# Where ScalarE's queue holds the transfers of constants at the start of an encoder kernel: in front of the splits of x, or traced behind them

## The chip, the cores and the metric

The kernel runs on one core of one Trainium2 chip. The metric is the device time of one execution in microseconds (us). The engines are named TensorE (PE, matrix products; its weight loads are PEld), VectorE (DVE), ScalarE (ACT), GpSimd (POOL) and SyncE (SP). Transfers between DRAM and the on-chip memory are issued by SyncE and ScalarE here.

## The reference

Two layers of an encoder over 256 tokens of width 1024, in float32. Each layer is a feed-forward half step, a token mixer, and a second feed-forward half step:

```python
x = x + 0.5 * swiglu(rms_norm(x, norm_ffn1[l]), ffn1_in[l], ffn1_out[l])
h = rms_norm(x, norm_mix[l])
proj = h @ w_in[l]      # RWKV-7 columns | attention columns | branch gates
...                     # o_a: bidirectional RWKV-7 scans; o_b: differential attention
y = jnp.einsum('bsgc,gcd->bsgd', branches, w_branch[l])
merged = jnp.sum(gates * y, axis=2)
x = x + merged @ w_out[l]
x = x + 0.5 * swiglu(rms_norm(x, norm_ffn2[l]), ffn2_in[l], ffn2_out[l])
```

`rms_norm(x, g)` is x times its gain g, divided by the root of the mean square of x over the features.

## The kernel before

Activations stay on chip with the feature in the partition: `x` has 8 feature tiles of 128 partitions by 256 tokens. Weights stream through once, in tiles of 128 x 1024 (512 KB). A product in float32 is made of three passes in the type float32r: each operand is split into a high and a low part (`xh`, `xl` of x; `wh`, `wl` of a weight tile), and `mm3` (L145 to L147) adds xh·wh, xl·wh and xh·wl.

`weights` (L131) issues a weight tile's transfer on SyncE into `wr` (three buffers), then ScalarE makes `wh` (L135, three buffers) and VectorE makes `wl` (L139, two buffers).

`x_ready` (L150) handles one feature tile of x. ScalarE writes gain · x into `xh` (L158), VectorE writes the rest into `xl` (L159), ScalarE squares x (L162 for the first tile, L165 for the others), and from the second tile on GpSimd adds the square to a sum (L166, the last statement). `rstd` (L169) takes the sum over features, forms the reciprocal root `rsT`, puts it on a diagonal with `ident` (L179), spreads it over the partitions with a matmul (L181), and ScalarE copies the outcome to `rs` (L183). The feed-forward multiplies each product by `rs` only when it reads the accumulator (L199), so that matmuls can start before `rs` is there; three accumulators (`acc`) exist.

`run` (L842) issues the transfer of the first layer's packed vectors `vec` on SyncE, calls `constants`, then `x_ready` for the 8 tiles with a lowered rank for the squares (XP = -300), and then the layers. `constants` (L98) fills `ones` and `mhalf`, issues x in two transfers (256 KB and 768 KB) and six transfers of constants, all on ScalarE's queue: `ident` (L108), the second layer's `vec` (L110), `masks` (L112), `cum` (L114), `dist` (L116) and `hind` (L118). The transfers `lora`, `lra` and `lng` of `rwkv_common` (L263 to L267) are on the same queue and are traced behind the first feed-forward stage.

The program's order is set by the planner of the framework (Tile). The code is traced into a list; the planner then walks through modelled time and gives each engine, of the instructions that are ready, the one of the highest rank, which by default is the place in the trace. `high_priority(n)` shifts the rank. `issue_after(i)` adds an order (no wait for completion) behind instruction `i` for those instructions traced in its block that run on the engine of `i`. Each engine then works its queue strictly in that order.

Of the kernel before, what the change touches and what calls it, by code (L numbers as in the profile page):

```python
"""Hybrid bidirectional encoder trunk: macaron SwiGLU halves around RWKV-7 and differential attention.

Activations stay feature-major on chip ([feature in partition, feature tile, token]); weights stream
once. Float32 products of the large matrices are carried by float32r passes over an exact split of
both operands into a high and a low part.
"""
# [19 lines left out]
D = 1024  # L26
S = 256
L = 2
KD = D // P
# [11 lines left out]
XP = -300  # L41
# [3 lines left out]

# tiles that share a place with others
PLACE = {"b0": "ar0", "b1": "ar1", "b2": "wt0", "b3": "wt1", "b4": "ab", "b5": "qb", "ak2": "x"}

# columns of the packed vectors
V_F1, V_MIX, V_F2, V_MU, V_A0, V_KK, V_KA, V_RK, V_LB, V_QG, V_KG, V_SG = (  # L50
# [4 lines left out]
class Trunk:  # L55
# [21 lines left out]
    def slot(self, tag, shape, dt=F32, half=False):  # L77
        """A tile of 8 KB (or 4) in a partition; tiles of one tag follow each other in place."""
        tag, n = PLACE.get(tag, tag), int(np.prod(shape[1:]))
        t = self.sp.tile([P, 1024 if half else 2048], dt, tag=tag, name=self.nm(tag))  # L80
        v = t[:, :n]
        names = "abcd"[:len(shape) - 1]
        if len(names) > 1:
            v = v.rearrange(f"p ({' '.join(names)}) -> p {' '.join(names)}", **dict(zip(names, shape[1:])))
        return v
# [13 lines left out]
    def constants(self):  # L99
        nc, io = self.nc, self.io  # L100
        self.ones = self.cp.tile([P, P], F32, name="ones")
        nc.vector.memset(self.ones, 1.0)
        self.mhalf = self.cp.tile([P, 32], F32, name="mhalf")
        nc.scalar.activation(self.mhalf, self.ones[:, 0:32], AF.Copy, scale=-0.5)
        self.ident = self.cp.tile([P, P], F32, name="ident")
        nc.scalar.dma_start(self.x[:, 0:2], io["x"][:, 0:2])
        nc.scalar.dma_start(self.x[:, 2:8], io["x"][:, 2:8])
        nc.scalar.dma_start(self.ident, io["c_ident"])  # L108
        for l in range(1, L):
            nc.scalar.dma_start(self.vec[l], io["vec"][l])  # L110
        self.masks = self.cp.tile([P, 6, 64], F32, name="masks")
        nc.scalar.dma_start(self.masks, io["c_masks"])  # L112
        self.cum = self.cp.tile([P, 2, 130], F32, name="cum")
        nc.scalar.dma_start(self.cum, io["c_cum"])  # L114
        self.dist = self.cp.tile([P, 384], F32, name="dist")
        nc.scalar.dma_start(self.dist, io["c_dist"])  # L116
        self.hind = self.cp.tile([P, 2], F32, name="hind")
        nc.scalar.dma_start(self.hind, io["c_hind"])  # L118
        self.da = self.cp.tile([P, S], F32, name="da")
        self.sdg = self.cp.tile([P, S], F32, name="sdg")  # L120
        self.lng = self.cp.tile([P, 4, 64], F32, name="lng")
        self.mu1 = self.cp.tile([P, 15], F32, name="mu1")
        self.mu2 = self.cp.tile([P, 15], F32, name="mu2")
        self.ka1 = self.cp.tile([P, 4], F32, name="ka1")
        self.kah = self.cp.tile([P, 4], F32, name="kah")
        self.a0h = self.cp.tile([P, 8], F32, name="a0h")

    # weights ------------------------------------------------------------------------------------
    def weights(self, src, n):
# [18 lines left out]

    # the residual and its norm ------------------------------------------------------------------
    def x_ready(self, l, g0, k, start, later=0):  # L150
        """Splits gain * x of one feature tile and adds its squares."""
        nc = self.nc
        x, g = self.x[:, k], self.vec[l][:, g0 + k:g0 + k + 1]
# [30 lines left out]

    # feed-forward half step ---------------------------------------------------------------------
    def ffn(self, l, w_in, w_out, nxt):
# [30 lines left out]

    # one tile of x @ W for two feature tiles, in a bank -----------------------------------------
    def project(self, w_in, tiles):
# [7 lines left out]
    def shifted(self, l, tiles, outs):  # L227
        """outs = p + mu * (centred_shift(p) - p) of RWKV column tiles."""
        nc, n = self.nc, len(tiles)
# [23 lines left out]

    # RWKV-7: everything that the scans need -----------------------------------------------------
    def rwkv_common(self, l):
        """The low-rank parts and the places of what the pairs of heads give."""
        nc, io, vec = self.nc, self.io, self.vec[l]
# [42 lines left out]
    def rwkv_kr(self, l, p):  # L300
        """Key and receptance of a pair of heads."""
        self.shifted(l, [4 + p, p], [self.kr[:, p, 0], self.kr[:, p, 1]])

    def rwkv_v(self, l, q):
        """Values of two pairs of heads, by token."""
        nc = self.nc
        v = self.tmp("vv", [P, 2, S], bufs=1)
        self.shifted(l, [8 + 2 * q, 9 + 2 * q], [v[:, 0], v[:, 1]])
        for i in range(2):
            ps = self.gen()  # L310
            for c in range(4):
                self.turn(ps[:, c * 64:c * 64 + 64], v[:, i, c * 64:c * 64 + 64])
            nc.scalar.activation(self.vt[:, 2 * q + i], ps[:, :S].rearrange("p (c s) -> p c s", c=4), AF.Copy)

    def rwkv_pair(self, p):
        """A pair of heads in both directions; the last part of the second direction waits for the next call."""
        st = self.pair_front(p, self.kr[:, p, 0], self.kr[:, p, 1])
# [15 lines left out]
    def turn(self, out, a):  # L333
        """out[h] = a[h].T for both halves of the partitions."""
        for h in range(2):
# [3 lines left out]
    def pair_front(self, p, k, r):  # L339
        nc, vec, mm = self.nc, self.vl, self.nc.tensor.matmul  # L340
        # kk = k * k_k; its squared norm's reciprocal by head goes into kk * iclr
        kk, sq = self.t1(), self.t1()
# [17 lines left out]
    def unit_front(self, p, d, st, sig, a2, da):  # L360
        nc, mm = self.nc, self.nc.tensor.matmul
        k, r, kk, bm, ks = st
        c4 = lambda t: t.rearrange("p (c s) -> p c s", c=4)
        # 2 * iclr - 1 = tanh of half the logit
        a, bw, kd = self.t1(), self.t1(), self.t1()
# [31 lines left out]
    def unit_back(self, p, d, st, bw, kw):  # L397
# [26 lines left out]
        if d == 1:  # L424
            # sum over a head of r * r_k * (k of both directions)
            ps = self.gen()
# [6 lines left out]

    # (I - A)^-1 of the 32 x 32 diagonal blocks, one in a partition ---------------------------------
    def invert(self, q):
# [24 lines left out]

        # 16 x 16 blocks, row by row from below: X[i, j:] = G[i, j:] X[j:, j:]
        D16 = 16 * 33
        nc.vector.tensor_copy(view(x, 14 * 32 + 15, (D16, 2), (1, 1)), view(g, 14 * 32 + 15, (D16, 2), (1, 1)))
        for i in range(13, -1, -1):
# [3 lines left out]
            add(view(x, i * 32 + j, (D16, 2), (1, n)), tm)  # L468
        # the block off the diagonal: X01 = X00 G01 X11, with X00 G01 in the place below G's diagonal
        for o in range(0, 16, 4):  # L470
# [18 lines left out]
    def merge_blocks(self, q):  # L489
        """The blocks off the diagonal: T = D + D A D."""  # L490
        nc, dt = self.nc, self.dt[q]
# [15 lines left out]

    # the scans, chunk by chunk --------------------------------------------------------------------
    def chain(self, l, q):
        """Two pairs of heads, both directions: the forward scan at chunk j, the other at chunk 3 - j."""  # L510
        nc, mm = self.nc, self.nc.tensor.matmul
# [96 lines left out]

    # differential attention -----------------------------------------------------------------------
    def att(self):  # L610
# [55 lines left out]
    def attention_core(self, l):  # L666
# [3 lines left out]
        for h in range(4):  # L670
# [13 lines left out]
            for m in range(2):  # L684
                for t in range(2):
                    nc.scalar.activation(lg[m][:, t], lg[m][:, t], AF.Exp, scale=slope, bias=mx[:, m, t:t + 1],
                                         accum_out=sm[:, m, t:t + 1])
            # e0 / s0 - lambda * e1 / s1 = (e0 - lambda * s0 / s1 * e1) / s0
            nc.vector.reciprocal(rs, sm)
# [30 lines left out]

    # the token mixer ------------------------------------------------------------------------------
    def gates(self, l, b):
        """2 * sigmoid - 1 = tanh of half the logits, kept in DRAM until the branch is ready; a step a feature tile."""
        nc = self.nc
# [31 lines left out]
    def gated(self, q, n0, r):  # L756
        """Weights of a filler: their split is queued behind the inversion's steps."""
        ops, n = self.inv[q], [0]
# [83 lines left out]
    def run(self, stages):  # L842
# [4 lines left out]
        self.constants()  # L847
        for k in range(KD):
            self.x_ready(0, V_F1, k, k == 0, XP)
        outf = lambda j: nc.scalar.dma_start(io["out"][:, j], self.x[:, j])  # L850
# [70 lines left out]
```

## Time and profile before

| | |
|---|---|
| time, median of 3 runs | 1410.89 us (1405.38 to 1413.88) |
| profiled execution, first to last instruction | span 1406.5 us (no time of its own is given beside it) |
| TensorE busy | 1349.9 us, 96% |
| VectorE, ScalarE, GpSimd busy | 67%, 47%, 20% |
| data moved | 227.60 MB, 162 GB/s mean |
| TensorE clock granted, mean | 0.987 |

A share of busy time is a mean over stages. The span has seven stages between the six instructions that write `rs`: a head of 27.1 us, and then feed-forward and mixer stages in turn.

### The profile page before, as it was taken

How to read it: one execution, taken by the hardware profiler on the slowest of the kernel's cores; microseconds unless marked ns; L12 is line 12 of the kernel's file. 1: busy time of each engine (PE TensorE's matmuls, PEld its weight loads, DVE VectorE, ACT ScalarE, POOL GpSimd, SP SyncE). 2: the span in 40 equal slices, each digit the busy share in tenths (PEclk: the TensorE clock that was granted, in tenths of full speed). 3: DMA queues.
4: the chain of work that ended last, by engine and by line, in shares of the span. 5: the costliest groups of instructions: out<-in, count | busy, mean ns of one | idle time of the engine just before them, and what ended most of it. 6: DMA issues, size and time to landing. Idle time of an engine off the chain costs nothing.

```text
span 1406.5 us, 30996 instructions
## 1 busy us (share of the span) xinstructions
PE 1349.9 (96%) x12916; PEld 1285.0 (91%) x12916; DVE 940.7 (67%) x1421; ACT 664.8 (47%) x1059; POOL 288.2 (20%) x284
## 2 busy tenths in 40 slices
PE   6999999998989999999999999999988999999999
PEld 6999998877889899999999999988767888999998
DVE  4655557799957766555556655588999577656644
ACT  5444445344444455444444444554543554544432
POOL 3111015445001112111111111154540010211100
PEclk9999999999999999999999999999999999999999
DMA  6555664325333565556655556633352445555564
GB/s 230 182 181 182 180 207 156 99 91 138 108 103 116 191 229 177 185 181 179 181 184 187 183 174 183 218 111 113 93 143 83 114 136 193 175 187 184 183 188 143
DMA packets 90333, 227.60 MB, mean 162 GB/s; under 512 B 29264, under 2 KB 35408, under 8 KB 89680
## 3 DMA queue, kind: packets, MB, share of 16 engines
q1 hardware_dynamic: 78640, 207.16, 47.0%
q10 hardware_dynamic: 11552, 18.46, 3.9%
q8 instruction: 101, 1.65, 0.5%
q14 instruction: 40, 0.33, 0.1%
HBM read 214.05 MB, written 11.53 MB: 160 GB/s over the span
## 4 chain that ended last, share of the span: by engine, by line
PE 80%; DVE 11%; DMA 3%; issue 2%; ACT 2%; POOL 2%; ACTq 0%; SPq 0%; DVEq 0%; POOLq 0%
PE acc L147 23%; PE acc L146 23%; PE acc L145 23%; DVE tv L458 3%; DVE wl L139 3%; DVE lora L459 2%; PE back L331 1%; PE gen L331 1%; PE att L679 1%; PE back L337 1%; PE gen L283 1%; DMA x<-xd 1%; DMA x<-x 1%; DMA f<-g 0%; PE acc L643 0%
## 5 line engine op out<-in xcount | busy, mean ns | idle before, releaser
L135 ACT ACTIVATE wh<-wr 128x1024 fp32r<-128x1024 f32 (+1 forms) x390 | 404.9, 1039 | 414.7 <-PE acc L146 268.6
L139 DVE TENSOR_TENSOR wl<-wr,wh 128x1024 fp32r<-128x1024 f32 (+1 forms) x390 | 475.5, 1219 | 171.0 <-PE acc L147 83.0
L145 PE MATMUL acc<-xh,wh 128*128 128x256 f32 x1904 | 540.2, 286 | 11.8 <-ACT wh L135 11.8
L146 PE MATMUL acc<-xl,wh 128*128 128x256 f32 x1904 | 539.5, 285 | 0.0
L147 PE MATMUL acc<-xh,wl 128*128 128x256 f32 x1904 | 529.9, 286 | 2.4 <-DVE wl L139 2.1
L145 PEld LDWEIGHTS acc<-xh,wh 128*128 128x128 f32 x1904 | 367.0, 193 | 17.3 <-ACT wh L135 12.0
L146 PEld LDWEIGHTS acc<-xl,wh 128*128 128x128 f32 x1904 | 367.0, 193 | 3.2 <-issue 2.5
L147 PEld LDWEIGHTS acc<-xh,wl 128*128 128x128 f32 x1904 | 360.6, 193 | 9.4 <-issue 3.5
L204 POOL TENSOR_TENSOR t<-t,t 128x256 f32<-128x256 f32 x88 | 89.3, 1016 | 403.7 <-ACT t L202 403.7
L145 PE MATMUL acc<-ar,wh 128*128 128x256 f32 x512 | 144.9, 283 | 0.0
L147 PE MATMUL acc<-ar,wl 128*128 128x256 f32 x512 | 144.9, 283 | 0.0
L199 DVE TENSOR_TENSOR t<-acc,rs 128x512 f32<-128x512 f32 x88 | 60.8, 692 | 119.7 <-PE acc L147 114.6
L146 PE MATMUL acc<-wt,wh 128*128 128x256 f32 x384 | 108.9, 284 | 0.0
L145 PEld LDWEIGHTS acc<-ar,wh 128*128 128x128 f32 x512 | 98.3, 192 | 0.0
L147 PEld LDWEIGHTS acc<-ar,wl 128*128 128x128 f32 x512 | 98.3, 192 | 0.0
L145 PE MATMUL acc<-wt,wh 128*128 128x256 f32 x320 | 91.0, 286 | 3.4 <-DVE x L839 2.2
L166 POOL TENSOR_TENSOR vv<-vv,t 128x256 f32<-128x256 f32 x42 | 36.8, 876 | 279.4 <-ACT t L165 271.8
L147 PE MATMUL acc<-wt,wl 128*128 128x256 f32 x320 | 91.5, 286 | 1.3 <-DVE wl L139 1.2
L458 DVE TENSOR_TENSOR tv<-lora 64x8 f32<-64x8 f32 (+10 forms) x88 | 74.9, 852 | 1.9
L146 PEld LDWEIGHTS acc<-wt,wh 128*128 128x128 f32 x384 | 74.4, 194 | 0.0
L146 PE MATMUL acc<-ab,wh 128*128 128x256 f32 x256 | 72.4, 283 | 0.0
L145 PEld LDWEIGHTS acc<-wt,wh 128*128 128x128 f32 x320 | 61.9, 194 | 4.0 <-issue 2.4
(234 smaller groups left out, 1935.1 us busy)
## 6 DMA issues: line engine op xcount, KB each, us to landing
wr<-f1i SPq DMA_DIRECT2D x88, 512.0 KB, 3.7
wr<-f2i SPq DMA_DIRECT2D x88, 512.0 KB, 3.6
wr<-win SPq DMA_DIRECT2D x62, 512.0 KB, 3.6
wr<-f1o SPq DMA_DIRECT2D x32, 512.0 KB, 3.6
wr<-f2o SPq DMA_DIRECT2D x32, 512.0 KB, 3.6
wr<-watt SPq DMA_DIRECT2D x24, 512.0 KB, 3.7
wr<-wbr SPq DMA_DIRECT2D x16, 512.0 KB, 3.6
wr<-wout SPq DMA_DIRECT2D x16, 512.0 KB, 3.4
```

The costliest lines, as they stand in the source:

```text
L135: nc.scalar.activation(wh[:, :n], raw[:, :n], AF.Copy)
L139: nc.vector.tensor_tensor(wl[:, :n], raw[:, :n], wh[:, :n].bitcast(F32), ALU.subtract)
L145: mm(out, wh, xh, start=first, stop=False)
L146: mm(out, wh, xl, start=False, stop=False)
L147: mm(out, wl, xh, start=False, stop=last)
L166: nc.gpsimd.tensor_tensor(self.sq, self.sq, sq, ALU.add)
L199: nc.vector.tensor_tensor(gu, ps.rearrange("p (a b) -> p a b", a=2), self.rs.unsqueeze(1).to_broadcast([P, 2, S]), ALU.mult)
L204: nc.gpsimd.tensor_tensor(h, s, gu[:, 1], ALU.mult)
L283: mm(ps, dw[r, t * P:(t + 1) * P], w2[r], start=True, stop=True)
L331: self.nc.tensor.matmul(out[r], a[r], b[r], start=start, stop=stop)
L458: mul = lambda o, a, b: ops.append(nc.vector.tensor_tensor(o, a, b, ALU.mult).ins)
L459: add = lambda o, a: ops.append(nc.vector.tensor_reduce(o, a, AX.X, ALU.add).ins)
```

## The change

The loop over `x_ready` moves from `run` into `constants`, behind the two transfers of x. The six transfers of constants (and the allocation of the tiles behind them) become a new function, `constants_late`, which is called behind the loop, in a block of `issue_after` with the last instruction traced so far. Nothing else changes but comments that are left out.

```diff
         nc.scalar.dma_start(self.x[:, 0:2], io["x"][:, 0:2])
         nc.scalar.dma_start(self.x[:, 2:8], io["x"][:, 2:8])
+        for k in range(KD):
+            self.x_ready(0, V_F1, k, k == 0, XP)
+        with self.tc.issue_after(nc.cur_bb.bb.instructions[-1]):
+            self.constants_late()
+
+    def constants_late(self):
+        nc, io = self.nc, self.io
         nc.scalar.dma_start(self.ident, io["c_ident"])
         for l in range(1, L):
             nc.scalar.dma_start(self.vec[l], io["vec"][l])
...
         self.constants()
-        for k in range(KD):
-            self.x_ready(0, V_F1, k, k == 0, XP)
         outf = lambda j: nc.scalar.dma_start(io["out"][:, j], self.x[:, j])
```

## Rows read from the trace of the kernel before

**Rows 1.** The page: busy us of each engine, and the chain that ended last.
```profile
PE 1349.9 (96%) x12916; PEld 1285.0 (91%) x12916; DVE 940.7 (67%) x1421; ACT 664.8 (47%) x1059; POOL 288.2 (20%) x284
...
PE 80%; DVE 11%; DMA 3%; issue 2%; ACT 2%; POOL 2%; ACTq 0%; SPq 0%; DVEq 0%; POOLq 0%
```

**Rows 2.** Stages: from:to, us, busy us (instructions) per engine, clock, DMA share, GB/s.
```profile
0.00:27.10 27.10, 14.74 (x98) 13.93 (x99) 12.38 (x23) 13.18 (x25) 8.40 (x12) 1.00 0.72 246
27.10:218.04 190.94, 190.94 (x1592) 190.89 (x1591) 109.44 (x131) 91.96 (x131) 31.75 (x32) 1.00 0.59 188
218.04:528.00 309.96, 292.62 (x3274) 260.81 (x3272) 249.71 (x448) 148.92 (x269) 81.10 (x78) 0.96 0.43 134
...
719.28:910.82 191.54, 191.54 (x1597) 191.49 (x1596) 110.17 (x131) 90.96 (x130) 30.38 (x32) 1.00 0.59 188
910.82:1223.31 312.49, 288.90 (x3275) 257.01 (x3274) 250.66 (x442) 148.55 (x269) 85.19 (x78) 0.98 0.42 129
```

**Rows 3.** Timeline of TensorE: start, us, instruction, idle time before it and its releaser.
```profile
11.06 0.58 PE L145 MATMUL acc<-xh,wh 128*128 128x256 f32 x1 [11.06 <-ACT wh L135]
...
12.32 0.58 PE L147 MATMUL acc<-xh,wl 128*128 128x256 f32 x1 [0.47 <-DVE wl L139]
...
17.80 0.38 PE L145 MATMUL acc<-xh,wh 128*128 128x256 f32 x1 [0.75 <-ACT wh L135]
```

**Rows 4.** Timeline of the queues of SyncE (SPq) and ScalarE (ACTq, ACT), the head.
```profile
0.73 0.42 ACTq L106 DMA_DIRECT2D x<-x  x1
...
1.17 31.15 SPq L133 DMA_DIRECT2D wr<-f1i  x10
...
1.25 0.39 ACTq L107 DMA_DIRECT2D x<-x  x1
...
3.94 0.33 ACTq L112 DMA_DIRECT2D masks<-c_masks  x1
...
7.83 0.34 ACTq L116 DMA_DIRECT2D dist<-c_dist  x1
8.77 0.33 ACTq L118 DMA_DIRECT2D hind<-c_hind  x1
9.15 0.51 ACT L158 ACTIVATE xh<-x,vec 128x256 fp32r<-128x256 f32 x1 [6.45 <-DMA x<-x]
9.54 0.33 ACTq L263 DMA_DIRECT2D lora<-w  x1
9.57 0.49 ACT L158 ACTIVATE xh<-x,vec 128x256 fp32r<-128x256 f32 x1
9.97 1.04 ACT L135 ACTIVATE wh<-wr 128x1024 fp32r<-128x1024 f32 x1
```

**Rows 5.** Transfers: queue, count, KB each, us from issue to landing.
```profile
wr<-f1i SPq DMA_DIRECT2D x1, 512.0 KB, 6.6
x<-x ACTq DMA_DIRECT2D x1, 256.0 KB, 3.2
...
x<-x ACTq DMA_DIRECT2D x1, 768.0 KB, 7.5
ident<-c_ident ACTq DMA_DIRECT2D x1, 64.0 KB, 8.6
...
wr<-f1i SPq DMA_DIRECT2D x88, 512.0 KB, 3.7
```

**Rows 6.** Timeline of VectorE: the diagonal (L179) and reads of accumulators (L199).
```profile
23.25 0.48 DVE L179 TENSOR_SCALAR t<-ident,rsT 128x128 f32<-128x128 f32 x2 [0.83 <-POOL rsT L176]
...
27.52 1.29 DVE L199 TENSOR_TENSOR t<-acc,rs 128x512 f32<-128x512 f32 x2 [1.73 <-ACT rs L183]
...
39.57 0.69 DVE L199 TENSOR_TENSOR t<-acc,rs 128x512 f32<-128x512 f32 x1 [1.08 <-PE acc L147]
...
45.33 0.69 DVE L199 TENSOR_TENSOR t<-acc,rs 128x512 f32<-128x512 f32 x1 [1.50 <-PE acc L147]
```

**Rows 7.** Instructions that read `hind`, the earliest: count, duration in ns, first to last start.
```profile
L347 PEld LDWEIGHTS gen<-hind,t x32: 186/192/192, 233.9 to 996.0; 128*128 128x128 f32 x32
```

## The prediction

> **What bounds the kernel now.** I read the page first, then the span cut into stages, and then only the first 40 us, where the change lies. The page [rows 1] shows TensorE busy for 1349.9 us, 96% of the span, and 80% of the chain that ended last is TensorE. The reader is to see that ScalarE (47%) and the transfers are not the bound, so a change to them pays only where TensorE is seen waiting.
>
> The stages [rows 2] are cut at the six instructions that write the row scale `rs` (L183). The first feed-forward stages of the two layers take 190.94 and 191.54 us with TensorE busy throughout. The two mixers take 309.96 and 312.49 us, with 17 and 24 us of TensorE idle. The head, up to the first `rs`, has TensorE busy for 14.74 of 27.10 us. So 12.4 us are missing there, and this is all that the change can reach directly; it is 0.9% of the span.
>
> What fills those 12.4 us: TensorE's first matmul is at 11.06 and waited for `wh`, the high part of the first weight tile; 0.47 and 0.75 us follow in two further gaps [rows 3]. So 11.06 us is the head of the program before TensorE has anything.
>
> ScalarE's timeline of that head [rows 4] has two transfers of x (0.73, 1.25), `ident` and the second layer's `vec`, `masks` (3.94), `cum`, `dist` (7.83), `hind` (8.77), and only then the first split `xh` at 9.15, a second at 9.57, and `wh` at 9.97 to 11.01. The issues are not slow (0.33 to 0.42 us each); they wait. The landing times [rows 5] say for what. The first part of x lands at 0.73 + 3.2 = 3.93, and `masks` starts at 3.94. The first weight tile, issued at 1.17 [rows 4], lands 6.6 us later at 7.8, and `dist` starts at 7.83. The second part of x lands at 1.25 + 7.5 = 8.75, and `hind` starts at 8.77. Eight transfers (vec, two of x, three of weights, `ident`, vec) are out by then; from the ninth on, each seems to start as an earlier one lands. ScalarE works its queue in order, so the split of the first two tiles of x, whose data was there at 3.93, starts 5.2 us later, behind `dist` and `hind`.
>
> **The change, part by part.** No instruction is added or removed. Six transfers (`ident`, `vec`, `masks`, `cum`, `dist`, `hind`; by their shapes 64 + 33 + 192 + 130 + 192 + 1 = 612 KB) are traced behind 8 `xh` and 8 squares on ScalarE, 8 `xl` on VectorE and 7 adds on GpSimd. The vec of layer 0 and the weight tiles on SP's queue keep their place.
>
> *Does the hold bind?* `issue_after(i)` orders those instructions of its block that run on the engine of `i`. The last one traced in front of the block is `x_ready`'s last statement, the add on GpSimd (L166); the six transfers are issued by ScalarE. So I read the hold as empty. What is left is trace order, a rank among instructions that are ready at one moment. The trace shows how much readiness outweighs it: `lora` (L263), traced a whole feed-forward stage later, is issued at 9.54, ahead of the second split [rows 4]. The constants need nothing, the splits need x. So `ident`, `vec` and probably `masks` and `cum` still go out first, and only what is left once the planner counts x as landed changes place with the first splits.
>
> *What it can give.* Nothing, if the order stays. If `xh` 0 and 1 pass `dist` and `hind`, but `wh` stays behind `hind`, `wh` starts where the first `xh` does now, 9.15 in place of 9.97: 0.8 us. If all constants leave the head, `wh` is bound by its own tile at 7.83, ends 1.04 us later at 8.87, and TensorE starts at 8.9: 2.2 us. Beyond that, the constants that are in flight before 7.83 (64 + 33 + 192 + 130 = 419 KB) could slow x and weights by at most their own time, 419 KB at the head's 246 GB/s [rows 2] = 1.7 us, so the gain is at most 3.9 us. TensorE's matmuls at 11.06 and 12.32 last 0.58 us, that at 17.80 lasts 0.38 [rows 3]; I take it that the slow stretch moves with the start. I take 0.8 us, as the row of `lora` says that ready transfers stay in front.
>
> *What it can cost.* Each issue takes up to 0.42 us of ScalarE's queue, six of them about 2.5 us. `lora`'s issue (9.54 to 9.87) overlaps the splits at 9.15 to 9.66 and 9.57 [rows 4], so an issue beside an ACTIVATE costs near nothing; I take 0, and keep 2.5 us as the other end. Behind a moved transfer stand the squares and the next `wh`, for one of which TensorE already runs dry at 17.80 [rows 3]. Without the cover of the ACTIVATEs these 2.5 us would go straight into that gap.
>
> *Who needs the constants.* `ident` alone is due early: it enters the diagonal at 23.25 [rows 6]. From there come `rs` at 27.1 and the reads of the first two accumulators at 27.52, over by 28.8. Three accumulators exist, and a product takes 5.76 us (45.33 − 39.57 [rows 6]); the fourth product, which is read at 39.57, thus starts near 33.8. So `ident` may come about 5 us late for free, near 28. It took 8.6 us to land at worst [rows 5], so it must be issued after 19.6 to cost anything. The other constants are first read at 233.9 or later [rows 7]. I take 0.
>
> The Trainium skill, DMA: Bandwidth & Descriptors, section Rules for kernel authors, says to issue a transfer early, compute, and wait for it late; the change does the opposite. By the rule the constants would only lose by moving. The 5 us under `ident` and 200 us under the rest say that this loss is covered here, and the rule takes no account of the issue standing in front of compute, which is the cost that [rows 4] show.
>
> *The rest of the program.* The planner places instructions by modelled time, so a shift at the head may turn the order of work 300 us later. The trace prices this: the same stage, planned anew in the other layer, differs by 0.6 us in the feed-forward halves and by 2.5 us in the mixers [rows 2]. Two mixers turned the same way are 5 us (an estimate from these two rows), of either sign. I take 0, since 190 us of a feed-forward stage with no TensorE gap lie between.
>
> **Sum.** The profiled execution has a span of 1406.5 us; the runs shown have a median of 1410.89 (1405.38 to 1413.88), 4.4 us more, so I apply the difference to the median. 1410.89 − 0.8 + 0 + 0 = 1410.1 us, with −3.9 and +2.5 us as the ends of the head alone. The three runs spread over 0.6% by themselves; 0.5% (7 us) is about what a measurement here can tell from no change.
>
> **Rivals.** *It does nothing.* The order at the head stays: 1410.9. For it: an empty hold, and transfers that are ready at once. Against it: x may count as landed before `dist`. *It does what it says.* All six go behind the splits: 1407.0 to 1408.7. For it: rows 4 show 5 us of blocked queue. Against it: the hold is on another engine. *Slower: late constants wait in the queue of the weight splits.* By then three weight tiles are always in flight, and a transfer that must wait for one to land waits up to 3.7 us, the median of the weight tiles [rows 5], holding the next `wh` back; TensorE then runs dry. One such wait is within the gap won at the start; from two uncovered waits on (7.4 us) it decides: 1418, and 1425 with four. Against it: `lora` was issued like this at 9.54, beside the splits, and TensorE's wait for the next `wh` was 0.75 us [rows 3, 4]. The Trainium skill's rule of issuing early (DMA: Bandwidth & Descriptors, Rules for kernel authors) stands on this rival's side. *The mixers turn over.* 1401 to 1421 for twice the 5 us above. For it: 41 us of idle TensorE there, set by the order; against it: the two layers agree within 2.5 us.
>
> **How the numbers follow.** Forecast (0 to 2.2 us gained at the head, the rest as before) 0.48; nothing 0.14; full gain 0.10; late constants 0.08; mixers turned 0.20. The first three (0.72) lie within 0.5%, less 0.03 that the spread of the runs may carry out of it (0.02 faster, 0.01 slower). Of the turned mixers I put 0.10 below −0.5%, 0.06 above and 0.04 between; of the late constants 0.06 above and 0.02 between. Faster 0.10 + 0.02 = 0.12, slower 0.06 + 0.06 + 0.01 = 0.13, same 0.69 + 0.04 + 0.02 = 0.75. The range runs to 1401 and 1420, 10 us each way, and leaves out the far ends of the turned mixers and three or more waits. The likeliest case's own range is 1407 to 1413.
>
> **What would show it.** In the head: the place of the first `xh` in ScalarE's queue against `dist` and `hind` (forecast: ahead of at least one of them, near 4 to 8 us), the first matmul between 8.9 and 11.1, the diagonal with `ident` still near 21 to 24 with no wait for a transfer. In the stages: feed-forward within 1 us of 191, mixers within 3 us of 310 and 312.5. The prediction is wrong if the mixers move by over 5 us together, if TensorE shows new waits for `wh` between 12 and 40 us, or if the six transfers sit as a block behind the last square, which would mean that the hold binds.

## The result, and the profile after

The changed kernel takes 1425.86 us (1424.47 to 1427.58, 4 runs) against 1408.99 us (1405.38 to 1413.88, 4 runs) of the kernel before: a ratio of 1.0127, interval 1.0098 to 1.0155. It is slower by 17 us, outside the range that was given. The profiled execution took 1424.47 us with a span of 1422.7.

The page of the kernel after, busy time of each engine and the chain that ended last (before: [rows 1]):

```profile
PE 1362.4 (96%) x12916; PEld 1295.2 (91%) x12916; DVE 929.8 (65%) x1421; ACT 664.0 (47%) x1059; POOL 295.6 (21%) x284
...
PE 77%; DVE 12%; DMA 5%; POOL 2%; issue 2%; ACT 1%; SPq 0%; ACTq 0%; DVEq 0%; POOLq 0%
```

The instructions are the same in number, and TensorE is still at 96%. The page hides the loss: TensorE's busy time rose by 12.5 us for the same 12916 matmuls, while the mean granted clock fell from 0.987 to 0.977. The Trainium skill (Trainium Kernel Development and Optimization, Performance Expectations) calls matmul busy time a bad metric for how close a kernel is to its roofline, because matmuls are pipelined. Here it is no measure of a change either, with 96% on both sides of a loss of 1.3%, and the weight loads (PEld), with 91% on both sides, show no more.

The stages of the kernel after, cut at the writes of `rs` as in [rows 2] (from:to, us, busy us and instructions of PE, PEld, DVE, ACT, POOL, clock, DMA share, GB/s):

```profile
0.00:26.31 26.31, 15.19 (x98) 14.40 (x99) 12.06 (x23) 13.40 (x24) 8.37 (x12) 1.00 0.76 252
26.31:217.25 190.94, 190.94 (x1592) 190.89 (x1591) 109.17 (x131) 92.06 (x130) 30.11 (x32) 1.00 0.60 189
217.25:543.26 326.01, 299.41 (x3275) 265.61 (x3274) 244.21 (x448) 148.27 (x269) 90.28 (x78) 0.94 0.42 127
...
734.21:925.80 191.59, 191.59 (x1597) 191.54 (x1596) 108.94 (x131) 90.69 (x130) 31.25 (x32) 1.00 0.60 188
925.80:1239.46 313.66, 294.51 (x3275) 262.25 (x3274) 247.77 (x442) 148.13 (x270) 82.72 (x78) 0.96 0.42 129
```

[rows 2] cut the first mixer of the kernel before at 528.00, but `rs` is written at 528.34. Cut there, as the other stages are, it reads:

```profile
218.04:528.34 310.30, 292.96 (x3275) 261.12 (x3274) 249.71 (x448) 148.92 (x270) 81.10 (x78) 0.96 0.43 134
```

The head gained 0.79 us (27.10 to 26.31), the feed-forward stages stand still, the second mixer lost 1.2 us, and the first mixer lost 15.7 us (310.30 to 326.01). There TensorE is busy 6.5 us longer (299.41 against 292.96, at a clock of 0.94 against 0.96) and idle 9.3 us longer (26.6 against 17.3). In the second mixer it is busy 5.6 us longer, at a clock of 0.96 against 0.98, but idle 4.4 us less. So the change worked where it was made, and the loss stands 200 us behind it, in a stage that none of the moved transfers feeds late: `hind`, the last of them, was issued at 8.69.

The head after, ScalarE and its queue (before: [rows 4]; line numbers behind L107 are higher by 7 in the code that did not move):

```profile
1.66 0.45 ACTq L115 DMA_DIRECT2D ident<-c_ident  x1
...
4.10 0.51 ACT L165 ACTIVATE xh<-x,vec 128x256 fp32r<-128x256 f32 x1 [1.39 <-DMA x<-x]
...
4.47 0.47 ACTq L119 DMA_DIRECT2D masks<-c_masks  x1
...
7.91 0.33 ACTq L123 DMA_DIRECT2D dist<-c_dist  x1
8.69 0.33 ACTq L125 DMA_DIRECT2D hind<-c_hind  x1
9.07 1.06 ACT L142 ACTIVATE wh<-wr 128x1024 fp32r<-128x1024 f32 x1 [4.07 <-DMA x<-x]
```

The first two splits now start at 4.10 and 4.51 and not at 9.15 and 9.57, as soon as their part of x is there. `ident` still goes out first. In the planned queue both splits stand in front of the other five constants (`vec` goes out at 4.11 and no longer at 2.14, the others within 0.7 us of their old times), and `wh` still stands behind `hind`. The hold of `issue_after` is empty, as read: the six are issued by 8.69, while GpSimd's adds, the last of which is named in the hold, run until 20.3, and without the hold the planned program is the same to the last instruction.

The planned program also tells what the issues wait for. The framework gives the transfers eight semaphores in turn, and the issue of a ninth transfer waits for the landing of the first: `masks` for the first part of x, `dist` for the first weight tile, `hind` for the second part of x. The 5 us of blocked queue [rows 4] are these waits; they show no limit of the chip. TensorE's first matmul comes at 10.18 and not at 11.06 [rows 3]:

```profile
10.18 0.58 PE L152 MATMUL acc<-xh,wh 128*128 128x256 f32 x1 [10.18 <-ACT wh L142]
```

Where the first mixer loses is seen in TensorE's own timeline near its end. The kernel before, the last products of attention and the transposes of its output `osb` (start, us, instruction, idle time before it and its releaser):

```profile
457.71 0.61 PE L702 MATMUL att<-va,f 128*128 128x128 f32 x4
...
460.40 0.63 PE L716 MATMUL att<-ident,osb 128*128 128x128 f32 x4 [0.54 <-DVE osb L713]
...
463.97 0.63 PE L716 MATMUL att<-ident,osb 128*128 128x128 f32 x4 [0.42 <-DVE osb L713]
```

The kernel after, the same instructions:

```profile
468.72 0.71 PE L709 MATMUL att<-va,f 128*128 128x128 f32 x4
474.11 1.08 PE L723 MATMUL att<-ident,osb 128*128 128x128 f32 x4 [4.68 <-DVE osb L720]
477.23 1.11 PE L723 MATMUL att<-ident,osb 128*128 128x128 f32 x4 [2.04 <-DVE icl L726]
```

Attention's last product comes 11 us later. Before, other matmuls stood between those rows; after, nothing stands there in TensorE's queue. TensorE waits 4.68 and 2.04 us, and a group of four transposes then takes 1.1 us in place of 0.63. From the first of them to 483.5 the granted clock is 0.50, the lower of its two levels (1.2 in place of 2.4 GHz):

```profile
474.00:483.50 9.50, 7.35 (x43) 6.53 (x44) 4.64 (x13) 1.79 (x3) 1.98 (x2) 0.50 0.20 72
```

The second place lies earlier. SyncE's queue around the second block inversion, first the kernel before, then the kernel after (`d<-ab` writes its input to DRAM, `lora<-d` reads it back regrouped, `d<-lora` writes the first inversion's result):

```profile
334.35 0.33 SPq L440 DMA_DIRECT2D d<-ab  x1
336.97 2.74 SPq L450 DMA_DIRECT2D lora<-d  x4
...
343.27 0.50 SPq L480 DMA_DIRECT2D d<-lora  x1
```

```profile
341.50 0.42 SPq L447 DMA_DIRECT2D d<-ab  x1
342.96 0.51 SPq L487 DMA_DIRECT2D d<-lora  x1
...
346.51 0.93 SPq L457 DMA_DIRECT2D lora<-d  x2
...
350.67 1.02 SPq L457 DMA_DIRECT2D lora<-d  x2
```

The second inversion's input comes 7 us later, and two of its four reads stand behind other transfers. Which of these differences costs the 17 us, and whether they come from the moved transfers or from the order, the experiments had to say.

### The profile page after: what moved, and what is told of

Its sections match the earlier page's. It is cut to its first block, busy times and chain, and to the rows that moved or that the text cites. A ratio compares the mean times of both kernels' runs of the same rounds, so it can differ in the third digit from the quotient of the medians.

```text
span 1422.7 us, 30989 instructions
## 1 busy us (share of the span) xinstructions
PE 1362.4 (96%) x12916; PEld 1295.2 (91%) x12916; DVE 929.8 (65%) x1421; ACT 664.0 (47%) x1059; POOL 295.6 (21%) x284
## 4 chain that ended last, share of the span: by engine, by line
PE 77%; DVE 12%; DMA 5%; POOL 2%; issue 2%; ACT 1%; SPq 0%; ACTq 0%; DVEq 0%; POOLq 0%
PE acc L154 23%; PE acc L153 22%; PE acc L152 22%; DVE tv L465 3%; DVE wl L146 3%; DVE lora L466 2%; PE back L338 1%; DMA x<-xd 1%; PE gen L338 1%; DMA lora<-d 1%; DMA wr<-win 1%; POOL n L664 1%; PE att L686 1%; DMA wr<-wout 1%; PE gen L290 1%
## 5 line engine op out<-in xcount | busy, mean ns | idle before, releaser
L153 PEld LDWEIGHTS acc<-wt,wh 128*128 128x128 f32 x384 | 75.2, 196 | 0.0
L154 PEld LDWEIGHTS acc<-wt,wl 128*128 128x128 f32 x320 | 62.8, 196 | 2.9 <-DVE wl L146 2.9
```

The lines of the kernel that those rows point to most:

```text
L153: mm(out, wh, xl, start=False, stop=False)
L154: mm(out, wl, xh, start=False, stop=last)
```

## The experiments

Where an order is pinned, a table lists for each engine the instructions traced behind the head in the order in which they are to be issued, and an order edge without a semaphore is put between each and the next:

```diff
+def pin(tc, traced, table):
...
+    info = mybir.DependencyInfo(mybir.DependencyClass.NoSync, mybir.DependencyReason.DATA)
+    for code in table.values():
+        places = ...   # one engine's instructions, by their place in the trace
+        for p, q in zip(places, places[1:]):
+            tc.add_manual_dep(traced[q], traced[p].name, info, reason="pin")
...
         Trunk(ctx, tc, io).run(stages)
+        pin(tc, list(nc.cur_bb.bb.instructions), ORDER)
```

**Head or order.** Two crossed kernels: e1 has the head of the kernel after and, from the first feed-forward stage on, the order of the kernel before; e2 has the head of before and the order of after.

> The changed kernel, with the issue order of every engine behind the head (all that is traced from the first feed-forward stage on) held to that of the kernel before. Theory P (the loss is the planner's other order in the first mixer; the moved transfers themselves gain 0.8 us at the head): ratio to the kernel before 0.998 to 1.001, first matmul near 10.2 us, first mixer 309 to 311 us. Theory T (the moved transfers themselves cost: later landing, other contention, or a lower clock that follows from them): ratio stays near 1.013 and the first mixer near 326 us.

> The kernel before with its head untouched, and the issue order behind the head held to that of the changed kernel. Theory P: ratio 1.011 to 1.015, first matmul at 11.06 us, first mixer 324 to 328 us. Theory T: ratio 0.999 to 1.001, first mixer 310 us.

e1: 1407.07 us, ratio 0.9982 (0.9964 to 1.0001), first mixer 309.70 us. e2: 1425.61 us, ratio 1.0128 (1.0096 to 1.0159), first mixer 327.86 us. The first matmuls are at 9.98 (expected near 10.2) and 10.71 (expected at 11.06). The whole loss goes with the order, none with the moved transfers. Alone, they tend to a small gain, which the interval does not quite tell from nothing.

**How little it takes.** e3 moves one transfer of 1 KB:

```diff
-        self.hind = self.cp.tile([P, 2], F32, name="hind")
-        nc.scalar.dma_start(self.hind, io["c_hind"])
...
             self.x_ready(0, V_F1, k, k == 0, XP)
+        self.hind = self.cp.tile([P, 2], F32, name="hind")
+        nc.scalar.dma_start(self.hind, io["c_hind"])
```

> The kernel before, with only the last of the six constants, hind (1 KB, first read at 233.9 us), traced behind the splits of x; planned freely. Theory P: the planner turns the first mixer as in the changed kernel (GpSimd's order there is the same), so most of the loss comes with 1 KB: ratio 1.006 to 1.016, first mixer 318 to 328 us. Theory T: a sixth of the loss or less, ratio at most 1.003.

1429.66 us, ratio 1.0141 (1.0098 to 1.0185), first mixer 328.51 us. The move of 1 KB costs as much as that of 612 KB, and its head gains as much (`rs` at 26.39).

**A hold that binds.** e4 gives `issue_after` the last square on ScalarE, so that the constants do go out behind the splits; e5 is e4 with the order of the kernel before pinned behind the head.

```diff
-        with self.tc.issue_after(nc.cur_bb.bb.instructions[-1]):
+        last = next(i for i in reversed(nc.cur_bb.bb.instructions) if i.engine == mybir.EngineType.Activation)
+        with self.tc.issue_after(last):
```

> The changed kernel with the hold on ScalarE's own last instruction (the last square) instead of GpSimd's add, so that the six constants do stand behind the splits; planned freely, which gives a third order of the first mixer. Theory P: the first matmul comes at 8.9 to 9.5 us (1.6 to 2.2 us gained at the head), and the time goes by whatever the first mixer is planned to, 305 to 330 us; ratio 0.995 to 1.015. Theory T: more of the moved transfers' cost than in the changed kernel, ratio over 1.013, with waits for constants or for weights between 12 and 40 us.

> The hold on ScalarE's own last square, so that the six constants do stand behind the splits, with the order behind the head held to that of the kernel before. Theory P (only the mixer's order cost anything; a head with late constants costs at most 2 us): ratio 0.998 to 1.003, first matmul near 9.1 us, first rs at 26 to 28 us, first mixer 309 to 311 us. The rival that late constants cost by themselves (T): ratio over 1.005 with the head's end later than 219 us.

e4: 1425.87 us, ratio 1.0126 (1.0097 to 1.0156). e5: 1407.55 us, ratio 0.9984 (0.9959 to 1.0009). The first matmul is at 9.08 and 9.01, 2 us before its old place [rows 3]. In e4 that gain is gone again by `rs`, at 27.73. In e5 `rs` stands at 24.18, earlier than the 26 to 28 that were expected, and at the end of the first feed-forward stage 1.9 us are left of the gain (216.15 against 218.04). ScalarE's rows of e4, and TensorE's stretch from 18 us on (columns as in the stages above), show where its gain went:

```profile
10.08 0.34 ACTq L116 DMA_DIRECT2D ident<-c_ident  x1
...
14.83 2.95 ACT L143 ACTIVATE wh<-wr 128x1024 fp32r<-128x1024 f32 x3 [1.29 <-DMA lng<-lng]
```

```profile
18.00:21.40 3.40, 3.40 (x19) 3.40 (x18) 1.24 (x1) 0.00 (x0) 0.16 (x1) 0.50 0.72 234
```

In e4's queue the six constants stand behind the last square and in front of the second `wh`. The issue of `hind` waits until a transfer of `lng` has landed (the 1.29 us), so that this `wh` starts at 14.83; in e5, which has `lng` behind it, the same `wh` starts at 13.09. TensorE then waits 0.85, 0.45 and 0.23 us for the weight splits between 15.1 and 17.6, and runs at a granted clock of 0.50 from 18.0 to 21.4, where the kernel before has 1.00 from 16 us on. Even so, what the head wins is at most 0.2% here, and the order behind it takes 1.3%.

By itself e4 does not part the two theories: 1.0126 lies inside the range of P and a hair below that of T, and waits for `wh` did come. e5 does, by its ratio. Its profiled execution is the slowest of its ten (1415.29 us), and the first mixer takes 316.86 us in it, outside the 309 to 311 that were expected.

**Is it SyncE's queue?** e6 keeps the order of after on four engines and gives SyncE that of before.

> The changed kernel, with the order of the changed kernel held on TensorE, VectorE, ScalarE and GpSimd, and SyncE's queue alone held to that of the kernel before: in the first mixer the second inversion's transfers stand ahead of two weight tiles and of the first inversion's results. Theory S (SyncE's queue is where the loss arises): ratio 0.998 to 1.006. Theory C (the last unit of the scan's inputs is computed 7 us later, on GpSimd and VectorE, and SyncE's order only follows): ratio 1.009 to 1.014.

1426.32 us, ratio 1.0130 (1.0097 to 1.0164), first mixer 332.93 us. The four reads of the second inversion are together again, from 345.0 on, and nothing is won. Theory S falls.

**A rank near the turn.** e7 is the kernel after with the rank of one part, the last pair of heads' keys, changed:

```diff
-PR = {'k3': -150, 'B': 60}
+PR = {'k3': -50, 'B': 60}
```

> The changed kernel with the rank of the last pair's key and receptance (k3) lowered by 50 places in place of 150; planned freely. The plan has the second inversion's gather directly behind its first transfer again, as before. Theory C (a late last unit makes the loss): the second inversion's first transfer starts by 337 us and its result leaves by 393 us, first mixer 306 to 314 us, ratio 0.994 to 1.004. If the loss lies elsewhere in the order: those times come early and the mixer stays over 318 us.

1408.31 us, ratio 0.9998 (0.9978 to 1.0017). With the head of the kernel after the loss is gone: output transposes at 465.96 and 469.06 without the wait, first mixer 314.91 us, just over the range. The second inversion's input leaves at 338.15, later than the 337 that were expected, its result at 389.10. So the new head forces no bad plan; it tips the planner to one.

**Is it the late second inversion?** e8 puts attention's third tile copy behind the last pair's decay copies on ScalarE, and leaves the rest to the planner:

```diff
+        t, info = list(nc.cur_bb.bb.instructions), mybir.DependencyInfo(mybir.DependencyClass.NoSync, mybir.DependencyReason.DATA)
+        for p, q in ((2924, 2925), (2925, 3991)):
+            tc.add_manual_dep(t[q], t[p].name, info, reason="decays first")
```

> The changed kernel with two order edges on ScalarE in the first mixer: the copy of the attention's third tile (out of its accumulator) waits in the queue behind the two decay copies of the last unit; the rest is planned freely and falls into another order, with the second inversion's first transfer and gather ahead of two weight tiles, as before. Theory C: first transfer by 337 us, second result by 393 us, first mixer 306 to 314 us, ratio 0.994 to 1.004. Otherwise: ratio over 1.008.

1427.93 us, ratio 1.0142 (1.0111 to 1.0173): a miss. The second inversion's input leaves at 337.64, sooner than in e7, which does not lose, and its result at 389.81, as early as before (390.65); still the kernel is no faster. The first mixer takes 325.34 us, and in this plan the second one loses too (321.07 against 312.49). An early second inversion is thus not enough. TensorE's waits of e8 between 450 and 490 us (waiter, whom it waited for, us in total, times, longest) are those of the kernel after:

```profile
PE att L723 <- DVE osb L720: 4.8, 1, 4.8
PE att L723 <- DVE icl L726: 2.0, 1, 2.0
```

**Cutting the order in two.** A prefix of one plan can be followed by the rest of the other. e9 follows the plan of after up to the transposes of attention's second head, near 405 us, and then that of before; e10 the reverse.

> The kernel after with a written-out order: each engine follows the plan of the kernel after up to the transposes of attention's second head (there the first mixer stands near 405 us), and behind them the plan of the kernel before. Theory D (the loss arises in the late part: the last two attention heads come 10 us late, TensorE's other work is used up, and it waits for osb): near the kernel before, 1407 to 1413, the two osb transposes near 462 to 468 with under 1.5 us of wait, first mixer 310 to 317. Theory E (the loss is made in front of 405 us, in the inversions and the pairs, and the late wait only passes it on): 1420 to 1427, as the kernel after, first mixer 322 to 328.

> The counterpart: each engine follows the plan of the kernel before up to the transposes of attention's second head and behind them the plan of the kernel after. Theory D (the loss arises in the late part): 1418 to 1427, TensorE waits 4 us or more for osb and icl at the output transposes, first mixer 320 to 328. Theory E (the loss is made in front of 405 us): 1405 to 1411, first mixer 308 to 314, under 1.5 us of wait at those transposes.

e9: 1416.14 us, ratio 1.0061 (1.0040 to 1.0082). e10: 1412.14 us, ratio 1.0031 (1.0017 to 1.0045). Neither theory holds alone: each part carries a loss of its own. The early one is the larger, against theory D. The windows 330 to 430 and 450 to 490 us (columns as in the stages above) of before, after, e9 and e10, in this order:

```profile
330.00:430.00 100.00, 92.09 (x1276) 81.92 (x1277) 80.86 (x134) 44.17 (x86) 8.96 (x8) 0.91 0.42 117
450.00:490.00 40.00, 37.86 (x396) 36.19 (x391) 30.59 (x58) 18.19 (x29) 4.63 (x5) 0.96 0.55 180
```

```profile
330.00:430.00 100.00, 87.31 (x1180) 76.43 (x1181) 73.63 (x126) 39.58 (x78) 14.32 (x11) 0.90 0.39 107
450.00:490.00 40.00, 32.77 (x350) 30.07 (x349) 26.16 (x56) 16.17 (x33) 5.07 (x5) 0.87 0.35 113
```

```profile
330.00:430.00 100.00, 86.56 (x1175) 76.67 (x1173) 72.02 (x124) 40.52 (x81) 12.81 (x9) 0.88 0.37 104
450.00:490.00 40.00, 37.87 (x432) 35.53 (x431) 29.57 (x60) 18.99 (x39) 4.62 (x5) 1.00 0.51 165
```

```profile
330.00:430.00 100.00, 93.75 (x1325) 83.39 (x1321) 81.89 (x140) 45.08 (x87) 11.25 (x8) 0.91 0.42 117
450.00:490.00 40.00, 33.50 (x332) 31.76 (x331) 26.27 (x52) 17.65 (x34) 5.07 (x5) 0.91 0.47 151
```

The reader is to see the first number in brackets, TensorE's matmuls. The busy time in front of it stretches with a lower clock: e1, in the order of before, has 1297 matmuls in the first window in only 88.75 us of busy time, at a clock of 0.98 against 0.91. After lacks 96 matmuls in the first window (1180 against 1276) and 46 in the second (350 against 396). e9 lacks them only in the first, e10 only in the second. TensorE's waits between 450 and 490 us say the same; e9, then e10:

```profile
PE att L723 <- DVE osb L720: 1.0, 2, 0.5
```

```profile
PE att L723 <- DVE osb L720: 3.5, 1, 3.5
PE att L723 <- DVE icl L726: 2.5, 1, 2.5
```

In the profiled executions the first mixer takes 318.83 us in e9 and 316.06 in e10, 9.1 and 6.4 us over e1's 309.70; together 15.5, where the kernel after has 16.3; each is from a single execution. In the times the two ratios make 0.92% of the 1.27%; the intervals leave open whether the rest needs both parts.

**Cutting the early part.** e11 follows after up to the last matmul that feeds the second inversion, near 341 us, and then before; e12 follows before up to there, after to the transposes of the second head, and before behind them.

> A written-out order that cuts the early part of e9 in two: the plan of the kernel after up to the last matmul that feeds the second inversion (near 341 us), and the plan of the kernel before from there to the end. If the 7.5 us of e9 are made in front of the second inversion (the last pair comes about 6 us late, VectorE then runs dry around 340 to 370): 1413 to 1419, the second inversion's first result issued near 343 and its first operands at 341. If they are made behind it (the order of inversion, decays and attention between 341 and 405): 1406 to 1411.

> The counterpart in three pieces: the plan of the kernel before up to the last matmul that feeds the second inversion, the plan of the kernel after from there to the transposes of attention's second head, the plan of the kernel before behind them. If e9's 7.5 us are made in front of the second inversion: 1406 to 1411. If they are made between 341 and 405 us: 1413 to 1419. If both need each other, this and the cut before it both lie under 1413, and their sum stays short of e9's loss.

e11: 1411.09 us, ratio 1.0028 (1.0016 to 1.0041). e12: 1418.76 us, ratio 1.0081 (1.0055 to 1.0108). The late input alone is the small part, although VectorE waits longest for it; VectorE's largest wait of e11 between 330 and 430 us:

```profile
DVE lora L470 <- DMA lora<-d: 6.8, 1, 6.8
```

The larger part lies in the order of the inversion, the decays and attention's first heads, between 341 and 405 us. The two do not add up to e9: 0.28% and 0.81% against 0.61%, which is little more than the intervals allow. Which instruction there costs most stays open; no run moved them one by one.

## Why the prediction was wrong

**The head was right.** The term of 0.8 us is what the profile shows: `rs` 0.79 us earlier, the first matmul 0.88. The hold is empty, the two splits pass `dist` and `hind` and not `ident`, with `wh` still behind `hind`, which is the case that gave the 0.8, and the diagonal with `ident` runs at 22.37 with no wait for a transfer. The forecast "If all constants leave the head … TensorE starts at 8.9" was tried by e4 and e5: 9.08 and 9.01. The issue cost, taken as 0, shows no loss in the kernel after.

Three readings were off, and none decides. `vec`, `masks` and `cum` were expected in front of the splits and stand behind them. The row of `lora`, on which the choice of 0.8 rests, was misread: in the planned queue `lora` stands behind two splits, the first `wh` and two squares, and its issue (9.54) only starts before they have run. So the right term came in part by luck. And the mixers of the kernel before differ by 2.2 us and not by 2.5, since [rows 2] cut the first one 0.34 us short.

**The late constants** did not come in the kernel after, and e5, whose constants are late in earnest, shows no loss to them beyond 0.2 us of its head's gain. e4 shows the mechanism of that rival, an issue in front of `wh` that waits for a landing, at 2.6 us (2.0 won at the first matmul, 0.6 lost at `rs`). The Trainium skill's rule to issue early (DMA: Bandwidth & Descriptors, Rules for kernel authors) stood on that rival's side; no wait of the kernel after or of e5 for a constant shows it at work. That this rival's 1425 for four waits is the measured time is chance.

**The step that failed** is "The rest of the program": "Two mixers turned the same way are 5 us … I take 0, since 190 us of a feed-forward stage with no TensorE gap lie between." The mechanism was named there and as the rival that the mixers turn over, with 0.20 and a range that ends at 1421; its size and its likelihood were off. It measured +15.7 us in the first mixer and +1.2 in the second, against 2.5 us each. Two arguments broke. The difference between the layers is no price of a new plan: it compares two orders that happen to take about the same time, and says nothing of a third. And a feed-forward stage without a gap keeps a shift of the head from reaching the mixer (in e1, with the old order, it takes 309.70 us against 310.30), but does not keep the planner from turning it: the written-out orders of e1 and e2 are the same in the feed-forward stages, but for a few neighbours at the start of the first, and differ in the mixers, where e2 puts the loss. It turns for 1 KB (e3), and a rank takes the loss away again (e7).

**Where the 17 us go**, by the ratios of e9 and e10: 0.61% of the 1.27% in front of 405 us, around the second inversion, and 0.31% behind, where attention's last product is 11 us late and TensorE's queue holds nothing to cover the wait. The other 0.35% belong to neither part, and the intervals do not tell them from nothing. That the order brings the last heads later is seen; why the planner's model preferred it was not tested and stays open.

No kernel here beats the one before beyond its interval: e1 (0.9982) and e5 (0.9984) come closest, and both need the written-out order.

## What to carry to other kernels

In a kernel whose order is planned by modelled times, an edit at one end is priced by the plan that it makes, so compare the planned order of all engines before believing a local sum, and do not price a new plan by how well two existing ones agree. The idle time of a stage (17 and 24 us in the mixers here) bounds what a new order can win there at the same clock; no row of the kernel before bounds what it can lose. The orders run here took between 309.70 and 332.93 us in the first mixer. To tell an edit from its plan, cross them: new code in the old order and old code in the new order. And a wait that stands out in a losing stage need not be the loss: the 6.8 us of VectorE in e11 go with 0.28%, and e8, which has no such wait in that window, loses 1.42%.

## What was not expected

The granted clock takes part in a loss by order: in the window from 450 to 490 us it is 0.96 before, 0.87 after, and 1.00 in e9, whose late order is that of before. TensorE's waits in the kernel after, 4.68 and 2.04 us, stand around the start of the stretch at 0.50 (474.0 to 483.5), whose matmuls take 0.41 us each (480 to 483 us); from 484 us on they take 0.28 us again. e4's head has the same sequence: three waits, then 0.50.

The same written-out order does not run alike twice in detail: the first mixer took 309.70 us in e1's profiled execution and 316.86 in e5's, the slowest of its ten, behind heads that differ by 1.9 us, while the medians of the two kernels lie 0.5 us apart. A stage of a single execution is thus good to some us, and the verdicts above rest on the ratios.
